# The last row tile of a normalised MLP output: another product order, its last product in two column halves, its store in quarters

## The chip, the cores and the metric

The kernel runs on one core of one Trainium2 chip. The metric is device time in microseconds (us) of one execution; lower is better. Five engines work side by side: TensorE (PE, matrix products, with its weight loads listed as PEld), VectorE (DVE), ScalarE (ACT), GpSimd (POOL) and SyncE (SP, which here issues transfers). Each takes its instructions in a fixed order and waits on semaphores that other engines or transfers raise. Products land in PSUM banks of 128 x 512 float32; the other tiles lie in SBUF. A row in this document that begins with a time, such as 1529.76, gives the start in us from the start of the profiled span.

## The reference, cut to what matters

Each of the DEPTH layers (one here) adds a token mixer and an MLP to x; then a last RMSNorm gives the output. Only the end bears on the change:

```python
def rms_norm(x, gain):
    xf = x.astype(jnp.float32)
    y = xf * lax.rsqrt(jnp.mean(xf * xf, axis=-1, keepdims=True) + NORM_EPS)
    return (y * gain.astype(jnp.float32)).astype(x.dtype)
...
        h = rms_norm(x, norm_mlp[l])
        x = x + jnp.square(jax.nn.relu(h @ w_up[l])) @ w_down[l]
    return rms_norm(x, norm_final)
```

x is 1024 x 1024 float32 (SEQ x D_MODEL), w_down is 4096 x 1024.

## The kernel before, in words

Rows of x are cut into eight row tiles of 128. The product of the MLP's hidden rows with w_down is not taken block by block: each 2 x 2 arrangement of blocks is computed with seven products in place of eight (Strassen's scheme in Winograd's form). A pair `pr` of row tiles, `pr` and `pr + 4`, is the upper and the lower half of such an arrangement; the two column halves of 512 are its other axis. `PLAN` names for each of the seven steps the PSUM bank that accumulates (X, Y or Z) and the two operands; `ADDS` says for each step into which column half `ci` and which row tile `pr + 4 * cj` VectorE then adds or subtracts the bank. Banks go on accumulating over steps: X is read after steps 0, 2, 4 and 6, Y after 1 and 5, Z after 3.

Every product is made of float32 operands split in a high and a low part: `mm3` issues three matmuls (lines 144, 145, 146) into the same bank. A step takes two blocks of the inner dimension, so six matmuls, each 128 x 512, for each row pair.

The inner dimension is walked in `n_kb` rounds of two blocks. The last round's second half (`alone`) takes its two pairs one after the other, pair 2 and then pair 3, all seven steps of each; before that, pairs go through the steps two at a time. Pair 3 (row tiles 3 and 7) thus comes last. In the order before, the last four additions of a pair (as `ADDS` has them) are, for pair 3, step 3 (Z into row 3, columns 0 to 511), step 4 (X into row 7, columns 512 to 1023), step 5 (Y into row 7, columns 0 to 511) and step 6 (X into row 3, columns 512 to 1023).

`finish(t, hf, whole)` is called when column half `hf` of row tile `t` is complete. At the first call for a row tile it multiplies that half by the final gain into `gx[:, 512:]` (line 1621, VectorE). At both calls ScalarE squares the half and sums it along the row (line 1624, with a read of the accumulator). At the second call (`whole`) VectorE adds the two sums (1626), ScalarE takes the root (1627), VectorE the reciprocal (1628); then VectorE scales the second half in place by reciprocal and gain (1629) while ScalarE scales the half that has its gain already (1632). ScalarE's queue issues the store of the one (1633), SyncE's the store of the other (1634), 256 KB each.

The order on each engine is made by the framework's list scheduler from the order of the code and its priorities; engines then keep to it. Waits are set by the framework from the tiles that an instruction reads and writes. All row tiles but rows 3 and 7 are stored while products of pair 3, or of pair 2, still run.

Of the kernel before, what the change touches and what calls it, by code (L numbers as in the profile page):

```python
# [18 lines left out]
P = 128  # L19
# [14 lines left out]
QUADS = 16  # L34
# [11 lines left out]
def trunk(ctx: ExitStack, tc: tile.TileContext, x, wts, mlp, pv, gains, mask_f, mask_u, out):  # L46
    nc = tc.nc
    V, A, G, PE = nc.vector, nc.scalar, nc.gpsimd, nc.tensor

    const = ctx.enter_context(tc.tile_pool(name="const", bufs=1))  # L50
# [11 lines left out]
    def bank(tag, name):  # L62
        return ps.tile([P, 512], F32, tag=tag, name=name, bufs={"pj": 4, "sc": 2, "hg": 2}[tag])
# [28 lines left out]
    def raw_tile(name):  # L92
        return wp.tile([P, 1024], F32, tag="raw", name=name, bufs=4)
# [44 lines left out]
    def pin(ins):  # L138
        if pinned[0]:
            tc.keep_in_program_order(ins)  # L140

    def mm3(o, ah, al, bh, bl, first, last, goes_on=False):
        how = {"skip_group_check": True} if goes_on else {}
        pin(PE.matmul(o, ah, bh, start=first, stop=False, **how))  # L144
        pin(PE.matmul(o, ah, bl, start=False, stop=False, **how))  # L145
        pin(PE.matmul(o, al, bh, start=False, stop=last, **how))  # L146
# [899 lines left out]
    for i in range(NC * NPAIR):  # L1046
# [398 lines left out]
    for part in range(2):  # L1445
# [4 lines left out]
        for hf in range(2):  # L1450
# [17 lines left out]
            for tt in tts:  # L1468
                cols = slice(hf * 512, (hf + 1) * 512)
# [36 lines left out]
    u_ops, last_u = {}, [None]  # L1506
# [70 lines left out]
    x2 = [(acc0, acc1)[t // 4].tile([P, D], F32, tag="acc", name=f"acc{t}", bufs=4) for t in range(8)]  # L1577
# [28 lines left out]
    for t in (0, 4, 1, 5, 2, 6, 3, 7):  # L1606
        nc.scalar.dma_start(x2[t], x2d[t])
    gain2 = gain_tile(2)
    ADDS = (
        ("X", 0, 0, ALU.add), ("Y", 1, 1, ALU.subtract), ("X", 0, 1, ALU.add), ("Z", 0, 0, ALU.add),  # L1610
        ("X", 1, 1, ALU.subtract), ("Y", 0, 1, ALU.add), ("X", 1, 0, ALU.subtract),
    )
    ssqs, with_gain = {}, {}

    def finish(t, hf, whole):

        cols = slice(hf * 512, (hf + 1) * 512)
        if t not in ssqs:
            ssqs[t] = const.tile([P, 2], F32, tag="ossq", name=f"ossq{t}", bufs=8)
            with_gain[t] = (raw_tile(f"gx{t}"), cols)  # L1620
            V.tensor_tensor(out=with_gain[t][0][:, 512:], in0=x2[t][:, cols], in1=gain2[:, cols], op=ALU.mult)
        ssq = ssqs[t]
        gx, cols_g = with_gain[t]
        A.activation(gx[:, 0:512], x2[t][:, cols], AF.Square, accum_out=ssq[:, hf : hf + 1])
        if whole:
            V.tensor_tensor(out=ssq[:, 0:1], in0=ssq[:, 0:1], in1=ssq[:, 1:2], op=ALU.add)
            A.activation(ssq[:, 0:1], ssq[:, 0:1], AF.Sqrt, bias=eps_t, scale=1.0 / D)
            V.reciprocal(ssq[:, 0:1], ssq[:, 0:1])
            V.scalar_tensor_tensor(
                x2[t][:, cols], x2[t][:, cols], ssq[:, 0:1], gain2[:, cols], op0=ALU.mult, op1=ALU.mult  # L1630
            )
            A.activation(gx[:, 512:], gx[:, 512:], AF.Identity, scale=ssq[:, 0:1])
            nc.scalar.dma_start(out[t * P : (t + 1) * P, cols_g], gx[:, 512:])
            nc.sync.dma_start(out[t * P : (t + 1) * P, cols], x2[t][:, cols])

    for kb in range(n_kb):
        last = kb + 1 == n_kb
        qs = order[2 * kb : 2 * kb + 2]
        for half in range(2):
            pairs = (2 * half, 2 * half + 1)  # L1640
            banks = {}
            if half == 1 and not last:
                nq = [QUADS + v for v in order[2 * kb + 2 : 2 * kb + 4]]
                for i in range(2):
                    load_quad(nq[i], raw_of[i], behind_late)
                    work[nq[i]] = quad_steps(nq[i], side[i][0], raw_of[i])
            alone = last and half == 1
            for step, (bk, wo, uo), prs in [
                (i, plan, prs) for prs in ([(pr,) for pr in pairs] if alone else [pairs]) for i, plan in enumerate(PLAN)
            ]:  # L1650
                first = (bk, prs[0]) not in banks
                for i, q in enumerate(qs):
                    wh, wl = ops_w[QUADS + q][wo]
                    uh, ul = u_ops[q][uo]
                    for pr in prs:
                        if first and i == 0:
                            banks[bk, pr] = bank(BANK[bk], f"d{bk}{kb}{pr}")
                        cut = slice(pr * P, (pr + 1) * P)
                        mm3(banks[bk, pr], uh[:, cut], ul[:, cut], wh, wl, first and i == 0, i == 1, not first)
                for pr in prs:  # L1660
                    _, ci, cj, op = ADDS[step]
                    dst = x2[pr + 4 * cj][:, ci * 512 : (ci + 1) * 512]
                    V.tensor_tensor(out=dst, in0=dst, in1=banks[bk, pr], op=op)  # L1663
# [90 lines left out]
```

## Time and profile before

| What | Before |
|---|---|
| time, median of 3 runs | 1540.57 us (1539.04 to 1540.85) |
| time of the profiled execution | 1539.23 us |
| its span | 1537.4 us |
| around the span | 1539.23 - 1537.4 = 1.83 us |
| PE busy | 1523.7 us, 99% of the span |
| VectorE, ScalarE busy | 1149.8 us (75%), 809.8 us (53%) |
| granted TensorE clock | 0.999 of full speed |
| start of the last product | 1529.33 us |

The span is what the profiler saw of the core, from its first to its last event; the time has 1.83 us more around it. A busy share is an average over the whole span. What happens after the last product is a stage of its own, in which PE does nothing; it is 1537.4 - 1529.33 = 8.1 us long, and it is read from the timeline, instruction by instruction, not from the shares.

### The profile page before, as it was taken

What the parts mean: (1) busy time and instruction counts of PE and PEld (TensorE: products, weight loads), DVE (VectorE), ACT (ScalarE), POOL (GpSimd) and SP (SyncE); (2) the same over time, 40 slices, a digit from 0 to 9 for tenths busy, and PEclk for the clock granted to TensorE, in tenths of its full rate; (3) what the DMA queues carried; (4) which work ended last, traced back from release to release, by engine and by line L of the source; (5) the groups of instructions that cost most, each with busy time, mean ns of one, the idle gap of its engine ahead of it and who ended that gap; (6) DMA issues with size and microseconds to landing.
All of it is one profiled execution on the core that took longest, in us unless ns stands there. A gap on an engine that the chain in (4) does not pass through costs nothing. (4 is left out here: it accounts for less than half of the span.)

```text
span 1537.4 us, 23195 instructions
## 1 busy us (share of the span) xinstructions
PE 1523.7 (99%) x9085; PEld 1274.5 (83%) x9085; DVE 1149.8 (75%) x1656; ACT 809.8 (53%) x1341; POOL 149.8 (10%) x188
## 2 busy tenths in 40 slices
PE   9999999999999999999999999999999999999997
PEld 7878988888889888888888888888888778888886
DVE  6798696485685838786856578888888898888877
ACT  6656757667567335454533357667776721111115
POOL 1021210232624600000000000000000000000000
PEclk9999999999999999999999999999999999999999
DMA  8545455465664374332339224766666675666642
GB/s 300 198 156 202 138 196 204 148 208 184 220 228 138 104 294 183 133 136 87 133 110 336 116 110 164 273 248 247 247 247 247 229 307 219 249 252 249 251 183 110
DMA packets 81679, 306.82 MB, mean 200 GB/s; under 512 B 8481, under 2 KB 20897, under 8 KB 68642
## 3 DMA queue, kind: packets, MB, share of 16 engines
q1 hardware_dynamic: 77536, 292.75, 51.8%
q10 hardware_dynamic: 4034, 12.59, 2.2%
q8 instruction: 71, 1.16, 0.3%
q14 instruction: 38, 0.31, 0.1%
HBM read 201.50 MB, written 103.81 MB: 199 GB/s over the span
## 5 line engine op out<-in xcount | busy, mean ns | idle before, releaser
L1663 DVE TENSOR_TENSOR acc<-acc,dX 128x512 f32<-128x512 f32 x128 | 85.2, 686 | 29.2 <-PE dX L146 26.7
L87 ACT CAST wA<-q 128x512 fp32r<-128x512 f32 x46 | 28.6, 621 | 146.6 <-PE dX L146 101.9
L88 DVE TENSOR_TENSOR wL<-raw,wH 128x1024 fp32r<-128x1024 f32 x46 | 56.3, 1226 | 41.1 <-ACT wH L87 40.8
L87 ACT CAST wH<-raw 128x1024 fp32r<-128x1024 f32 x46 | 48.2, 1050 | 34.4 <-DMA raw<-wts_in 14.3
L1663 DVE TENSOR_TENSOR acc<-acc,dY 128x512 f32<-128x512 f32 x64 | 43.5, 687 | 13.1 <-PE dY L146 12.9
L144 PE MATMUL po<-wH,y 128*128 128x512 f32 x128 | 49.9, 394 | 0.0
L145 PE MATMUL po<-wL,y 128*128 128x512 f32 x128 | 49.9, 390 | 0.0
L146 PE MATMUL po<-wH,y 128*128 128x512 f32 x128 | 49.7, 390 | 0.0
L1524 ACT ACTIVATE b<-b 128x512 f32<-128x512 f32 x48 | 30.2, 630 | 32.0 <-DVE b L1523 31.8
L88 DVE TENSOR_TENSOR wA<-q,wA 128x512 fp32r<-128x512 f32 x46 | 31.5, 687 | 16.2 <-ACT wA L87 15.8
L108 ACT CAST wH<-raw 128x1024 fp32r<-128x1024 f32 x36 | 37.7, 1048 | 8.3 <-issue 3.7
L569 DVE SCALAR_TENSOR_TENSOR xc<-xp,pvt,xc 128x512 f32<-128x512 f32 x48 | 40.2, 848 | 1.1 <-ACT xc L553 1.1
L175 POOL TENSOR_TENSOR rstd_h<-rstd_h,mhalf 128x1 f32<-128x1 f32 x8 | 4.6, 583 | 371.1 <-DVE rstd_h L170 371.1
L1085 DVE TENSOR_TENSOR s<-q,q 128x512 f32<-128x512 f32 x46 | 31.7, 688 | 3.9 <-DMA q<-mlp_in 3.5
L482 POOL TENSOR_TENSOR stt<-r,stt 128x256 fp32r<-128x256 f32 x16 | 19.8, 1261 | 126.4 <-ACT stt L481 114.2
L1093 DVE TENSOR_TENSOR s<-q 128x512 f32<-128x512 f32 x46 | 31.7, 688 | 0.4
L1525 ACT ACTIVATE b<-b 128x512 f32<-128x512 f32 x48 | 30.2, 631 | 1.2
L873 ACT ACTIVATE on<-po 128x128 f32<-128x128 f32 x64 | 16.8, 277 | 26.1 <-PE po L869 26.0
L146 PEld LDWEIGHTS po<-wH,y 128*128 128x128 f32 x128 | 24.0, 188 | 5.0
L144 PEld LDWEIGHTS po<-wH,y 128*128 128x128 f32 x128 | 24.1, 188 | 4.8
L145 PEld LDWEIGHTS po<-wL,y 128*128 128x128 f32 x128 | 24.1, 188 | 4.8
L1175 DVE TENSOR_TENSOR gb<-gY,ge 128x512 f32<-128x512 f32 x14 | 9.7, 691 | 23.6 <-PE gY L146 23.6
(2562 smaller groups left out, 5437.2 us busy)
## 6 DMA issues: line engine op xcount, KB each, us to landing
q<-mlp_in SPq DMA_DIRECT2D x92, 512.0 KB, 3.6
raw<-wts_in SPq DMA_DIRECT2D x80, 512.0 KB, 4.9
rest<-wL SPq DMA_DIRECT2D x36, 512.0 KB, 2.9
wL<-rest SPq DMA_DIRECT2D x36, 512.0 KB, 4.3
hd<-ri SPq DMA_DIRECT2D x16, 256.0 KB, 3.4
od<-onT ACTq DMA_DIRECT2D x8, 512.0 KB, 6.6
cdT<-stT SPq DMA_DIRECT2D x16, 256.0 KB, 3.1
o<-od SPq DMA_DIRECT2D x4, 1024.0 KB, 5.9
```

What stands on the lines that cost most here:

```text
L87: keep(A.copy(h, src))
L88: ins = V.tensor_tensor(out=lo, in0=src, in1=h.bitcast(F32), op=ALU.subtract)
L108: A.copy(h, raw)
L144: pin(PE.matmul(o, ah, bh, start=first, stop=False, **how))
L145: pin(PE.matmul(o, ah, bl, start=False, stop=False, **how))
L146: pin(PE.matmul(o, al, bh, start=False, stop=last, **how))
L569: ins = V.scalar_tensor_tensor(xc[:, s, :], xp[:, j : j + T], pvt[:, PV_CW + 8 * j + u : PV_CW + 8 * j + u + 1], xc[:, s, :], op0=ALU.mult ...
L1085: ins = V.tensor_tensor(out=sa[:, 0, :], in0=a21, in1=a22, op=ALU.add)
L1093: V.tensor_tensor(out=sb[:, 0, :], in0=a21, in1=a11, op=ALU.add)
L1524: A.activation(b[:, at, :], b[:, at, :], AF.Relu, scale=-1.0 if at == 2 else 1.0)
L1525: A.activation(b[:, at, :], b[:, at, :], AF.Square)
L1663: V.tensor_tensor(out=dst, in0=dst, in1=banks[bk, pr], op=op)
```

## The change

The change is in `finish` and in the last round's loop, and touches pair 3 alone (row tiles 3 and 7, the last ones):

- the steps of pair 3 run in the order 0, 1, 2, 4, 5, 3, 6: the two steps that complete row 7 (4 and 5) now stand ahead of step 3, which completes the first half of row 3;
- the last step, 6, is computed in two parts of 256 columns: six matmuls of 128 x 256 for columns 0 to 255 of the bank, an addition of 256 columns, a call of `finish`, and then the same for columns 256 to 511;
- `finish` with a `part` squares 256 columns only; the first part's sum is added to the sum of the row's other half in a tile of its own, `thirds`; the second part adds its own sum to that, and takes root and reciprocal;
- row 3 is then scaled and stored in four quarters of 256 columns (128 KB each): VectorE and ScalarE take a quarter each, twice; three of the stores are issued by SyncE, the fourth by ScalarE.

```diff
@@ finish
-        A.activation(gx[:, 0:512], x2[t][:, cols], AF.Square, accum_out=ssq[:, hf : hf + 1])
+        if part is None:
+            A.activation(gx[:, 0:512], x2[t][:, cols], AF.Square, accum_out=ssq[:, hf : hf + 1])
+        else:
+            if part == 0:
+                thirds[t] = const.tile([P, 2], F32, tag="thirds", name=f"thirds{t}", bufs=1)
+            now = slice(hf * 512 + part * 256, hf * 512 + part * 256 + 256)
+            o = thirds[t][:, 0:1] if part == 0 else ssq[:, hf : hf + 1]
+            A.activation(gx[:, part * 256 : part * 256 + 256], x2[t][:, now], AF.Square, accum_out=o)
+            if part == 0:
+                V.tensor_tensor(out=o, in0=o, in1=ssq[:, 1 - hf : 2 - hf], op=ALU.add)
+                return
         if whole:
-            V.tensor_tensor(out=ssq[:, 0:1], in0=ssq[:, 0:1], in1=ssq[:, 1:2], op=ALU.add)
+            other = ssq[:, 1 - hf : 2 - hf] if part is None else thirds[t][:, 0:1]
+            V.tensor_tensor(out=ssq[:, 0:1], in0=ssq[:, hf : hf + 1], in1=other, op=ALU.add)
             A.activation(ssq[:, 0:1], ssq[:, 0:1], AF.Sqrt, bias=eps_t, scale=1.0 / D)
             V.reciprocal(ssq[:, 0:1], ssq[:, 0:1])
+            if part is not None:
+                rows = slice(t * P, (t + 1) * P)
+                for i, dma in enumerate((nc.sync.dma_start, nc.scalar.dma_start)):
...
+                    V.scalar_tensor_tensor(
+                        x2[t][:, o], x2[t][:, o], ssq[:, 0:1], gain2[:, o], op0=ALU.mult, op1=ALU.mult
+                    )
+                    A.activation(gx[:, g], gx[:, g], AF.Identity, scale=ssq[:, 0:1])
+                    nc.sync.dma_start(out[rows, o], x2[t][:, o])
+                    dma(out[rows, o_g], gx[:, g])
+                return
@@ the loop of the last round
-                (i, plan, prs) for prs in ([(pr,) for pr in pairs] if alone else [pairs]) for i, plan in enumerate(PLAN)
+                (i, PLAN[i], prs)
+                for prs in ([(pr,) for pr in pairs] if alone else [pairs])
+                for i in ((0, 1, 2, 4, 5, 3, 6) if alone and prs[0] == 3 else range(7))
             ]:
+                if alone and prs[0] == 3 and step == 6:
+                    _, ci, cj, op = ADDS[step]
+                    for part in range(2):
+                        these = slice(part * 256, part * 256 + 256)
+                        o = banks[bk, 3][:, these]
...
+                            mm3(o, uh[:, cut], ul[:, cut], wh[:, these], wl[:, these], False, i == 1, True)
+                        dst = x2[3 + 4 * cj][:, ci * 512 + part * 256 : ci * 512 + part * 256 + 256]
+                        V.tensor_tensor(out=dst, in0=dst, in1=o, op=op)
+                        finish(3, ci, part == 1, part)
+                    continue
```

In the new file the addition of a bank stands in line 1703 (1663 before), that of a part in line 1689, the Square of a whole half in line 1625 and of a part in 1631, the sum for the root in 1637, the reciprocal in 1639, and row 3's quarter scalings in 1646 and 1649 with their stores in 1650 and 1651.

Every engine's instructions stand as before up to pair 3's last products. PE, the end of the program, before (dX, dY and dZ are the banks of pair 3; the operands named wA and ws are weights, u the hidden rows; a wait names the engine whose semaphore is awaited):

```order
L144 MATMUL dY_13595<-ws328H,u12B_13345 128x512
L145 MATMUL dY_13595<-ws328L,u12B_13345 128x512
L146 MATMUL dY_13595<-ws328H,u12B_13345 128x512
L144 MATMUL dY_13595<-ws329H,u13B_13353 128x512
L145 MATMUL dY_13595<-ws329L,u13B_13353 128x512
L146 MATMUL dY_13595<-ws329H,u13B_13353 128x512
L144 MATMUL dX_13587<-wA1228H,u12t_13347 128x512 [waits DVE_49]
L145 MATMUL dX_13587<-wA1228L,u12t_13347 128x512
L146 MATMUL dX_13587<-wA1228H,u12t_13347 128x512
L144 MATMUL dX_13587<-wA1229H,u13t_13355 128x512
L145 MATMUL dX_13587<-wA1229L,u13t_13355 128x512
L146 MATMUL dX_13587<-wA1229H,u13t_13355 128x512
```

PE, the same place now:

```order
L144 MATMUL dZ_13636<-wA1229H,u13B_13351 128x512
L145 MATMUL dZ_13636<-wA1229L,u13B_13351 128x512
L146 MATMUL dZ_13636<-wA1229H,u13B_13351 128x512
L144 MATMUL dX_13587<-wA1228H,u12t_13347 128x256 [waits DVE_49]
L145 MATMUL dX_13587<-wA1228L,u12t_13347 128x256
L146 MATMUL dX_13587<-wA1228H,u12t_13347 128x256
L144 MATMUL dX_13587<-wA1229H,u13t_13355 128x256
L145 MATMUL dX_13587<-wA1229L,u13t_13355 128x256
L146 MATMUL dX_13587<-wA1229H,u13t_13355 128x256
L144 MATMUL dX_13587<-wA1228H,u12t_13347 128x256 [waits DVE_49]
L145 MATMUL dX_13587<-wA1228L,u12t_13347 128x256
L146 MATMUL dX_13587<-wA1228H,u12t_13347 128x256
```

Z's products stand where Y's were; Y's have moved ahead of them. The last product's six matmuls have become twelve of half the width (the last three are not shown), and the second half's first one has a wait for VectorE: both halves lie in the bank dX_13587, and the semaphore count that it waits for is reached by VectorE's addition of the first half (L1689, below).

VectorE, the end of the program, before (acc_11405 is row tile 7, acc_11401 row tile 3, gx_13630 and gx_13619 their halves with gain, ossq_13629 and ossq_13618 their sums and scales):

```order
L1663 TENSOR_TENSOR acc_11401<-acc_11401,dZ_13610 128x512 [waits PE_49]
L1621 TENSOR_TENSOR gx_13619<-acc_11401,gain_11439 128x512 [waits DMAHW0_49,DVE_49]
L1663 TENSOR_TENSOR acc_11405<-acc_11405,dX_13587 128x512 [waits PE_49]
L1621 TENSOR_TENSOR gx_13630<-acc_11405,gain_11439 128x512 [waits DMAHW2_49,DVE_49]
L1663 TENSOR_TENSOR acc_11405<-acc_11405,dY_13595 128x512 [waits PE_49]
L1663 TENSOR_TENSOR acc_11401<-acc_11401,dX_13587 128x512 [waits PE_49]
L1626 TENSOR_TENSOR ossq_13629<-ossq_13629 128x1 [waits Activation_49]
L1626 TENSOR_TENSOR ossq_13618<-ossq_13618 128x1 [waits Activation_49]
L1628 RECIPROCAL ossq_13629<-ossq_13629 128x1 [waits Activation_49]
L1629 SCALAR_TENSOR_TENSOR acc_11405<-acc_11405,ossq_13629,gain_11439 128x512 [waits DVE_49]
L1628 RECIPROCAL ossq_13618<-ossq_13618 128x1 [waits Activation_49]
L1629 SCALAR_TENSOR_TENSOR acc_11401<-acc_11401,ossq_13618,gain_11439 128x512 [waits DVE_49]
```

VectorE, the same place now (ossq_13617 and gx_13618 are row 7's, ossq_13644 and gx_13645 row 3's):

```order
L1621 TENSOR_TENSOR gx_13618<-acc_11405,gain_11439 128x512 [waits DMAHW0_49,DVE_49]
L1703 TENSOR_TENSOR acc_11401<-acc_11401,dZ_13636 128x512 [waits PE_49]
L1637 TENSOR_TENSOR ossq_13617<-ossq_13617 128x1 [waits Activation_49]
L1689 TENSOR_TENSOR acc_11401<-acc_11401,dX_13587 128x256 [waits PE_49]
L1621 TENSOR_TENSOR gx_13645<-acc_11401,gain_11439 128x512 [waits DMAHW2_49,DVE_49]
L1639 RECIPROCAL ossq_13617<-ossq_13617 128x1 [waits Activation_49]
L1653 SCALAR_TENSOR_TENSOR acc_11405<-acc_11405,ossq_13617,gain_11439 128x512 [waits DVE_49]
L1633 TENSOR_TENSOR thirds_13655<-thirds_13655,ossq_13644 128x1 [waits Activation_49]
L1689 TENSOR_TENSOR acc_11401<-acc_11401,dX_13587 128x256 [waits PE_49]
L1637 TENSOR_TENSOR ossq_13644<-ossq_13644,thirds_13655 128x1 [waits Activation_49]
L1639 RECIPROCAL ossq_13644<-ossq_13644 128x1 [waits Activation_49]
L1646 SCALAR_TENSOR_TENSOR acc_11401<-acc_11401,ossq_13644,gain_11439 128x256 [waits DVE_49]
```

Both additions into row 7 (acc_11405) now come ahead of this piece. Between the two halves of row 3's last addition (L1689) VectorE now does the gain of row 3's first half, row 7's reciprocal, row 7's scaling (L1653) and the sum in `thirds`. One more quarter scaling follows the last row shown.

ScalarE, now, from row 7's second Square on:

```order
L1625 ACTIVATE gx_13645,ossq_13644<-acc_11401 128x512 [waits DMAHW2_49,DVE_49]
L1638 ACTIVATE ossq_13617<-ossq_13617,eps_t 128x1 [waits DVE_49]
L1631 ACTIVATE gx_13645,thirds_13655<-acc_11401 128x256 [waits DVE_49,Activation_49]
L1656 ACTIVATE gx_13618<-gx_13618,ossq_13617 128x512 [waits DVE_49]
L1657 DMA y_out<-gx_13618 128x512 [waits Activation_49]
L1631 ACTIVATE gx_13645,ossq_13644<-acc_11401 128x256 [waits DVE_49]
L1638 ACTIVATE ossq_13644<-ossq_13644,eps_t 128x1 [waits DVE_49]
```

Row 7's root, its scaling (L1656) and the issue of its store (L1657) stand ahead of the Square of row 3's second part; before, both rows' Squares stood ahead of both rows' roots.

More of the change, by code (lines that the diff above doesn't have):

```diff
@@ L1612, in trunk, with finish @@
     )
-    ssqs, with_gain = {}, {}
-    def finish(t, hf, whole):
+    ssqs, with_gain, thirds = {}, {}, {}
+    def finish(t, hf, whole, part=None):
         cols = slice(hf * 512, (hf + 1) * 512)
@@ L1623, in finish @@
         gx, cols_g = with_gain[t]
-        A.activation(gx[:, 0:512], x2[t][:, cols], AF.Square, accum_out=ssq[:, hf : hf + 1])
+        if part is None:
[9 more added lines that the diff above has]
+                return
         if whole:
-            V.tensor_tensor(out=ssq[:, 0:1], in0=ssq[:, 0:1], in1=ssq[:, 1:2], op=ALU.add)
+            other = ssq[:, 1 - hf : 2 - hf] if part is None else thirds[t][:, 0:1]
+            V.tensor_tensor(out=ssq[:, 0:1], in0=ssq[:, hf : hf + 1], in1=other, op=ALU.add)
             A.activation(ssq[:, 0:1], ssq[:, 0:1], AF.Sqrt, bias=eps_t, scale=1.0 / D)
             V.reciprocal(ssq[:, 0:1], ssq[:, 0:1])
+            if part is not None:
+                rows = slice(t * P, (t + 1) * P)
+                for i, dma in enumerate((nc.sync.dma_start, nc.scalar.dma_start)):
+                    g = slice(512 + 256 * i, 768 + 256 * i)
+                    o = slice(cols.start + 256 * i, cols.start + 256 * i + 256)
+                    o_g = slice(cols_g.start + 256 * i, cols_g.start + 256 * i + 256)
+                    V.scalar_tensor_tensor(
[5 more added lines that the diff above has]
+                return
             V.scalar_tensor_tensor(
@@ L1648, in trunk @@
             for step, (bk, wo, uo), prs in [
-                (i, plan, prs) for prs in ([(pr,) for pr in pairs] if alone else [pairs]) for i, plan in enumerate(PLAN)
+                (i, PLAN[i], prs)
+                for prs in ([(pr,) for pr in pairs] if alone else [pairs])
+                for i in ((0, 1, 2, 4, 5, 3, 6) if alone and prs[0] == 3 else range(7))
             ]:
                 first = (bk, prs[0]) not in banks
+                if alone and prs[0] == 3 and step == 6:
[3 more added lines that the diff above has]
+                        o = banks[bk, 3][:, these]
+                        for i, q in enumerate(qs):
+                            wh, wl = ops_w[QUADS + q][wo]
+                            uh, ul = u_ops[q][uo]
+                            cut = slice(3 * P, 4 * P)
+                            mm3(o, uh[:, cut], ul[:, cut], wh[:, these], wl[:, these], False, i == 1, True)
[3 more added lines that the diff above has]
+                    continue
                 for i, q in enumerate(qs):
```

## The prediction

> **What bounds the kernel now.** The page comes first: PE is busy in 99% of the span.
>
> ```profile
> span 1537.4 us, 23195 instructions
> PE 1523.7 (99%) x9085; PEld 1274.5 (83%) x9085; DVE 1149.8 (75%) x1656; ACT 809.8 (53%) x1341; POOL 149.8 (10%) x188
> ```
>
> The change neither removes nor adds column work on PE, so this share says nothing of it. What it touches is the stage behind the last products, and that is read from the timeline of the last 10 us (start, duration, engine, line, in square brackets the idle time and who ended it):
>
> ```profile
> 1529.33 0.39 PE L146 MATMUL dX<-wA1229H,u13t 128*128 128x512 f32 x1
> 1529.76 0.69 DVE L1663 TENSOR_TENSOR acc<-acc,dX 128x512 f32<-128x512 f32 x1 [0.67 <-PE dX L146]
> 1530.36 0.15 DVE L1626 TENSOR_TENSOR ossq<-ossq 128x1 f32<-128x1 f32 x1
> 1530.48 0.63 ACT L1624 ACTIVATE gx<-acc 128x512 f32<-128x512 f32 x1 [0.57 <-DVE acc L1663]
> 1531.01 0.19 ACT L1624 ACTIVATION_READ_ACCUMULATOR gx<-acc 128x1 f32 x1
> 1531.11 0.61 ACT L1627 ACTIVATE ossq<-ossq,eps_t 128x1 f32<-128x1 f32 x2
> 1531.23 0.16 DVE L1626 TENSOR_TENSOR ossq<-ossq 128x1 f32<-128x1 f32 x1 [0.72 <-ACT gx L1624]
> 1531.42 0.16 DVE L1628 RECIPROCAL ossq<-ossq 128x1 f32<-128x1 f32 x1
> 1531.62 0.75 DVE L1629 SCALAR_TENSOR_TENSOR acc<-acc,ossq,gain 128x512 f32<-128x512 f32 x1
> 1531.63 0.71 ACT L1632 ACTIVATE gx<-gx,ossq 128x512 f32<-128x512 f32 x1
> 1532.29 0.15 DVE L1628 RECIPROCAL ossq<-ossq 128x1 f32<-128x1 f32 x1
> 1532.37 0.37 ACTq L1633 DMA_DIRECT2D y_out<-gx  x1
> 1532.48 0.75 DVE L1629 SCALAR_TENSOR_TENSOR acc<-acc,ossq,gain 128x512 f32<-128x512 f32 x1
> 1532.78 0.72 ACT L1632 ACTIVATE gx<-gx,ossq 128x512 f32<-128x512 f32 x1 [0.45 <-DVE ossq L1628]
> 1533.54 0.34 ACTq L1633 DMA_DIRECT2D y_out<-gx  x1
> ```
>
> One sees a chain of single steps in which PE has no part: last addition, Square, root, reciprocal, and then two rows' scalings in a line, row 7's (1531.62) ahead of row 3's; the second reciprocal waits for VectorE to end row 7's scaling, and the second ScalarE scaling for the first one's issue as well. Last comes the transfer view of 1532.0 to 1537.4 (40 slices of 0.135 us, busy tenths of the transfer engines), and the stores' own view:
>
> ```profile
> DMA  0000000007999999999999999999400000000000
> DMA packets 576, 1.05 MB, mean 194 GB/s; under 512 B 64, under 2 KB 64, under 8 KB 576
> y_out<-gx ACTq DMA_DIRECT2D x1, 256.0 KB, 2.8
> L1634 SPq DMA_DIRECT2D y_out<-acc x8: 332/332/338, 1512.0 to 1533.3; - x8
> ```
>
> Four stores of 256 KB run in one block, slice 9 to slice 28, which is 1533.2 to 1535.9: 2.6 us, 0.8 us behind the first issue (1532.37). The last one, issued at 1533.54, has landed 2.8 us later, at 1536.34, 0.44 us behind the last bytes; the span ends 1.06 us after that. So the stage is bound twice: by the step chain up to 1533.54, and by 1 MB of stores that all start within it.
>
> **The change, term by term.** Up to the third X product of pair 3 every queue stands as before. From there:
>
> ```profile
> 1522.09 0.68 DVE L1663 TENSOR_TENSOR acc<-acc,dX 128x512 f32<-128x512 f32 x1
> 1523.17 0.39 PE L145 MATMUL dX<-ws128L,u12n 128*128 128x512 f32 x1
> 1524.08 0.39 PE L146 MATMUL dX<-ws129H,u13n 128*128 128x512 f32 x1
> 1524.31 0.39 PE L145 MATMUL dZ<-wA1228L,u12B 128*128 128x512 f32 x1
> 1524.51 0.69 DVE L1663 TENSOR_TENSOR acc<-acc,dX 128x512 f32<-128x512 f32 x1 [0.15 <-PE dX L146]
> 302.72 0.28 PE L145 MATMUL pv<-wL,hT10H 128*128 128x256 f32 x1
> 302.84 0.28 PE L146 MATMUL pv<-wH,hT10L 128*128 128x256 f32 x1
> ```
>
> PE, new order. Matmuls of 512 columns follow each other in 0.227 us (four steps from 1523.17 to 1524.08), those of 256 in 0.12 (302.72, 302.84). Twelve by 0.12 against six by 0.227 costs 1.44 - 1.36 = 0.08 us. A VectorE result releases PE 0.17 us after its end: 1522.09 + 0.68 = 1522.77, and the matmul behind the waiting one starts at 1523.17, one pitch after 1522.94. Four Y matmuls, in place of five Z ones, now fill the wait for the X addition that ends at 1524.51 + 0.69 = 1525.20; the next X matmul goes at 1525.37 instead of 1525.22, 0.15 late. Six X end their starts at 1526.50, two Y at 1526.96, five Z at 1528.09, six half-width ones at 1528.92; the first half's bank is complete at 1528.92 + 0.28 = 1529.20 and PE free at 1529.04.
>
> VectorE, the queue that decides. Rows for its pace:
>
> ```profile
> 1522.02 0.16 DVE L1626 TENSOR_TENSOR ossq<-ossq 128x1 f32<-128x1 f32 x1
> 1526.38 0.69 DVE L1621 TENSOR_TENSOR gx<-acc,gain 128x512 f32<-128x512 f32 x1
> 1527.04 0.69 DVE L1663 TENSOR_TENSOR acc<-acc,dX 128x512 f32<-128x512 f32 x1
> L664 DVE TENSOR_TENSOR dd<-sc,mf 128x256 f32<-128x256 f32 x8 | 3.4, 419 | 0.0
> L481 ACT CAST stT<-r 128x256 fp32r<-128x256 f32 x16 | 5.9, 416 | 0.7 <-POOL r L474 0.7
> ```
>
> Full-width additions follow at 0.66 us (1526.38, 1527.04), a sum of one column starts 0.60 behind an addition (1529.76, 1530.36), and an addition 0.07 behind such a sum (1522.02, 1522.09). Row 7's X addition can start at 1526.50 + 0.39 + 0.04 = 1526.93; Y's at 1527.59; the gain of row 7 at 1528.25; Z's addition at 1528.91; row 7's sum at 1529.51; the first half's addition at 1529.58, 0.42 long: 1530.00. PE, which waits for it since both halves lie in one bank, stands idle from 1529.04 to 1530.17 (1.13 us; behind the waiting matmul are only its five fellows), and has the second half ready at 1531.05. But VectorE isn't: the gain of row 3 (from 1529.93), row 7's reciprocal (1530.62; its root runs on ScalarE 1530.26 to 1530.55, behind the Square of row 3's first half), row 7's scaling (1530.82, 0.75) and the sum in `thirds` (1531.49) come first. The second half's addition runs 1531.56 to 1531.98. Before, the last addition ended at 1529.76 + 0.69 = 1530.45: **+1.53 us**. PE's wait is inside this; were it gone, row 7's work on VectorE would still end at the same time, so its price on the path is nothing.
>
> ScalarE. Row 7's scaling (1531.07 to 1531.78) and the issue of its store, which holds ScalarE 0.37 us (the [0.45] row above shows it), end at 1532.17; the last Square starts at 1532.21, not 1532.01: **+0.20**. A Square of 256 columns isn't in the trace; the cast of 256 took 0.416, the Square of 512 0.63, so it lies between 0.32 (half) and 0.63; I take 0.42, since cast and Square cost alike at 512 columns (0.62 and 0.63). Square start to scaling start took row 7 before 1531.62 - 1530.48 = 1.14 with its sum already made, and row 3 would have needed 1.46 (sum 0.19 more after 1531.23, root 0.31, reciprocal 0.20); less 0.21 it is 1.25: the first quarter's scaling starts at 1533.46. Row 3 before waited for row 7's scaling and started at 1532.48, 2.00 after its Square; here **-0.75**.
>
> Quarters. A 256-column scaling on VectorE lies between 0.38 (half) and 0.75; I take 0.48 (0.75 less the 0.27 that an addition saves, 0.69 to 0.42); on ScalarE 0.50. VectorE's end at 1533.93 and 1534.35, ScalarE's at 1533.96 and 1534.44. SyncE issues at 1533.95, 1534.30 and 1534.65 (0.33 each), ScalarE at 1534.47. The last issue starts 1.11 us later than the 1533.54 of before.
>
> Stores. Row 7's 512 KB are issued at 1531.6 and 1531.8 and are through by 1533.7, out of the way: this is what the new order buys. Row 3's four quarters begin at 1533.95 + 0.82 = 1534.77. Each has 128 rows of 1 KB, where the halves had 128 of 2 KB (512 such packets, 32 for each of 16 engines, in 2.62 us: 82 ns each). No row shows a 1 KB packet in this stage: it costs between 41 ns (bytes alone) and 82 ns. I take 41, because the block of before runs at 9 tenths throughout, as if bytes bound it: 32 packets by 41 ns is 1.31, last bytes at 1536.08, against 1535.9. **Sum: +0.2 us.** The span becomes 1537.6, this execution 1537.6 + 1.83 = 1539.4. The three runs' median is 1540.57, 1.34 above this execution; at the median I get 1540.8.
>
> [...] The trace has the last store's 2.8 us with three others ahead of it, and no lone quarter.
>
> **The rivals.** (1) *Faster*: the halves overlap and row 7 is out of the way, as the code is laid out. VectorE would then add the second half right behind the first, at 1530.42, and ScalarE take its Square at once: 1.56 + 0.20 sooner than above, last bytes at 1534.3, 1.6 before 1535.9. For it: ScalarE has 0.57 and 0.72 of idle time in the chain above. Against it: the rows of VectorE's queue, where four instructions of row 7 and row 3 stand between the halves, and PE's new wait, so the change does not do this. It gives 1537.6 in this execution, 1539.0 at the median. (2) *Slower*: a store's rows of 1 KB cost what rows of 2 KB do. Last bytes at 1534.77 + 2.62 = 1537.39, +1.5 us: 1540.7 here, 1542.1 at the median. It decides from 35 ns a packet on (1534.77 + 32 x 35 ns = 1535.9). For it: the fixed share of other small work here (256 columns cost 0.42 where 512 cost 0.69). (3) *Nothing at all*, the terms cancelling closer than I can reckon: 1540.57.
>
> **How the numbers follow.** The forecast and (3), which differ by 0.2 us, hold 0.65; (1), or a good part of it, 0.13; (2), or a good part, 0.22. About 0.2% (3.1 us) is what a measurement of this kernel can tell from no change, and the whole stage from the last product's start is 8.1 us; none of the cases leaves 0.2%. I leave 0.02 for faster and 0.04 for slower by more, for things outside this stage, so 0.94 for within. Bounds: the low ends (Square 0.32, scalings at half) save 0.2 on the way, the packet at 82 ns and full-width prices add 1.8; the runs of before lie 1.5 below and 0.3 above their median. The range takes (1) and (2) in: 1538.7 to 1542.5.
>
> **What would show it.** In the changed trace: PE idle near 1.1 us between the two halves, ended by VectorE's L1689; VectorE without a gap from 1526.9 to about 1532; row 7's scaling (L1653) ahead of the second L1689, which ends about 1.5 us later than 1530.45; the last issue near 1534.65; the block of four quarters 1.3 us long (2.6 in rival 2). If the second L1689 ends near 1530.5, rival 1 holds. If all ends before pair 3 have moved, the cause lies elsewhere and I am wrong altogether.

## The result, and the profile after

The changed kernel takes 1555.92 us (median of 4 runs, 1554.91 to 1557.12) against 1540.67 us of the kernel before (4 runs, 1539.04 to 1540.85): a ratio of 1.0101, 95% interval 1.0089 to 1.0113. It is 1.0% slower, by 15 us; the prediction had 1540.8 us and a range up to 1542.5. The profiled execution took 1556.85 us. Its page begins:

```profile
span 1555.0 us, 23218 instructions
PE 1539.8 (99%) x9091; PEld 1274.7 (82%) x9091; DVE 1152.3 (74%) x1659; ACT 811.3 (52%) x1344; POOL 153.7 (10%) x188
```

PE is busy 16.1 us longer (1523.7 before) with six matmuls more, and its share is still 99%. The granted clock is 0.999, as before. Outside its busy time PE has 1555.0 - 1539.8 = 15.2 us against 13.7, so waits are 1.5 us of the 17.6 us between the two spans. The rest is PE itself, slower at its work. (The two medians lie 15.25 us apart, the two profiled executions a little more.)

**The stage that was predicted.** To compare it I count from one instruction that is the same in both programs, the last X matmul ahead of the changed order (`dX<-ws129H,u13n`, line 146; 1524.08 before). In the timeline of the changed kernel:

```profile
1541.49 0.39 PE L146 MATMUL dX<-ws129H,u13n 128*128 128x512 f32 x1
...
1545.09 0.39 PE L144 MATMUL dZ<-wA1229H,u13B 128*128 128x512 f32 x1
1545.32 0.40 PE L145 MATMUL dZ<-wA1229L,u13B 128*128 128x512 f32 x1
1545.56 0.39 PE L146 MATMUL dZ<-wA1229H,u13B 128*128 128x512 f32 x1
...
1546.83 0.42 DVE L1689 TENSOR_TENSOR acc<-acc,dX 128x256 f32<-128x256 f32 x1
1547.30 0.39 PE L144 MATMUL dX<-wA1228H,u12t 128*128 128x256 f32 x1 [0.65 <-DVE acc L1689]
1548.02 0.75 DVE L1653 SCALAR_TENSOR_TENSOR acc<-acc,ossq,gain 128x512 f32<-128x512 f32 x1
1548.76 0.41 DVE L1689 TENSOR_TENSOR acc<-acc,dX 128x256 f32<-128x256 f32 x1
1549.23 0.42 ACT L1631 ACTIVATE gx<-acc 128x256 f32<-128x256 f32 x1 [0.42 <-DVE acc L1689]
1550.49 0.88 DVE L1646 SCALAR_TENSOR_TENSOR acc<-acc,ossq,gain 128x256 f32<-128x256 f32 x2
1551.90 0.45 SPq L1650 DMA_DIRECT2D y_out<-acc  x1
```

From the marker to the end of the span it was 1537.4 - 1524.08 = 13.32 us, and it is now 1555.0 - 1541.49 = 13.51: +0.19 us, where the prediction had +0.2. PE stands idle between the halves and VectorE ends the wait; row 7's scaling (1548.02) lies ahead of the second half's addition. All of it is there as told, and it is 1% of the loss. The marker itself starts 17.41 us later. Everything was lost before it, in code that the diff doesn't touch.

The transfers' view of the last 5.4 us of the changed kernel (40 slices of 0.135 us; moved GB/s below):

```profile
DMA  6999999899100000299459999999700000000000
GB/s 273 364 425 440 364 425 455 319 440 349 31 0 0 0 0 0 99 372 372 129 212 357 319 349 342 349 372 364 243 8 0 0 0 0 0 0 0 0 0 0
```

Row 7's stores are through before row 3's begin. Row 3's quarters are the block from slice 16 on: by the trace's packet records it runs from 1551.84 to 1553.58. There a packet of 1 KB takes 46 ns (median); one of 2 KB, in row 7's stores, takes 84.

**Where the time went.** The start of successive matmuls tells it: 1545.09, 1545.32, 1545.56 is a pitch of 0.235 us; before, 512 columns took 0.227. Windows of 200 us (columns: stretch, its length, PE busy and its matmuls, clock, share of the transfer engines, GB/s), of the kernel before, then of the changed one:

```profile
700.00:900.00 200.00, 200.00 (x908) 1.00 0.44 159
1300.00:1500.00 200.00, 200.00 (x884) 1.00 0.61 240
```

```profile
700.00:900.00 200.00, 200.00 (x891) 1.00 0.43 154
1300.00:1500.00 200.00, 200.00 (x872) 1.00 0.59 232
```

PE is busy without a gap at the same clock, and gets through 17 and 12 fewer matmuls. The transfers are not busier. Not every matmul is hit, though. Within one stage, the products into the bank gX (a row: line, operands, count, then shortest, median and longest duration in ns, first and last start), before and after:

```profile
L144 PE MATMUL gX<-gn2H,ws134H x4: 389/389/390, 561.8 to 563.9; 128*128 128x512 f32 x4
L144 PE MATMUL gX<-gT3H,ws334H x4: 389/389/390, 567.3 to 569.3; 128*128 128x512 f32 x4
```

```profile
L144 PE MATMUL gX<-gn2H,ws134H x4: 395/396/396, 562.7 to 564.8; 128*128 128x512 f32 x4
L144 PE MATMUL gX<-gT3H,ws334H x4: 389/389/390, 568.2 to 570.3; 128*128 128x512 f32 x4
```

Both weights lie in a pool on the left of SBUF. `gT3H` lies on the left too, `gn2H` in the pool `np`, which is opened with `side="right"`. Of these two only the product whose operands come from both sides has become slower. That points to where tiles lie. The diff makes one new tile, `thirds`, of 128 x 2 float32: 8 bytes in each partition. In the addresses of the compiled programs it takes 32 bytes in the pool `const`, and every pool that is opened on the left after it stands 32 bytes higher than before; the tiles on the right have not moved. Before, the start of the moving operand (512 columns) and that of the stationary one were a multiple of 512 bytes apart in all 512-column matmuls. Now 1872 of them have a distance of 32 bytes up or down of such a multiple. Pitch by stage, worked out from the starts in both traces (mean of the steps between successive 512-column matmuls, steps outside 0.20 to 0.26 us left out), and the count of matmuls times the difference:

| Products into | Matmuls | Before, ns | After, ns | Difference, us |
|---|---|---|---|---|
| pr, pi, g, mb (before 550 us) | 384 | 227.6 | 227.6 | 0.0 |
| gX, gY, gZ | 672, 336, 168 | 226.8, 226.7, 226.7 | 228.5, 230.2, 228.6 | 2.6 |
| po (820 to 918 us) | 384 | 226.9 | 230.3 | 1.3 |
| uX, uY, uZ | 768, 384, 192 | 227.1, 226.7, 226.9 | 233.3, 233.4, 233.3 | 8.5 |
| dX, dY, dZ | 768, 384, 192 | 226.9, 226.7, 227.0 | 230.2, 230.0, 229.5 | 4.3 |

The sum is 16.7 us, against 17.4 us by which the marker is late. PE's longer gaps are not in this sum, and they differ from profile to profile, by some 2.5 us in this case: the kernel before with an unused tile, of experiment 1, has the same pitches to 0.1 ns, and its marker, at 1539.03, is 14.95 us late. The products into dX, dY and dZ are slower too, though both operands of each come from one side; more of that below.

### The profile page after: what moved, and what is told of

Read it like the earlier page. It is cut to its first block, busy times and chain, and to the rows that moved or that the text cites. A ratio compares the mean times of both kernels' runs of the same rounds, so it can differ in the third digit from the quotient of the medians.

```text
span 1555.0 us, 23218 instructions
## 1 busy us (share of the span) xinstructions
PE 1539.8 (99%) x9091; PEld 1274.7 (82%) x9091; DVE 1152.3 (74%) x1659; ACT 811.3 (52%) x1344; POOL 153.7 (10%) x188
## 4 chain that ended last, share of the span: by engine, by line
PE 88%; DVE 7%; DMA 2%; issue 1%; ACT 1%; POOL 1%; SPq 0%; DVEq 0%; ACTq 0%
PE uX L144 4%; PE uX L145 4%; PE uX L146 4%; PE dX L144 3%; PE dX L146 3%; PE dX L145 3%; PE gX L144 3%; PE gX L145 3%; PE gX L146 3%; PE po L145 2%; PE po L146 2%; PE po L144 2%; PE pj_q L144 2%; PE uY L146 2%; PE uY L145 2%; PE uY L144 2%
## 5 line engine op out<-in xcount | busy, mean ns | idle before, releaser
L87 ACT CAST wH<-raw 128x1024 fp32r<-128x1024 f32 x46 | 48.2, 1048 | 34.1 <-DMA raw<-wts_in 15.2
L88 DVE TENSOR_TENSOR wA<-q,wA 128x512 fp32r<-128x512 f32 x46 | 31.6, 688 | 17.4 <-ACT wA L87 17.4
```

What stands on the lines that cost most here:

```text
L87: keep(A.copy(h, src))
L88: ins = V.tensor_tensor(out=lo, in0=src, in1=h.bitcast(F32), op=ALU.subtract)
```

## The experiments

The theory (**placement**): the new tile, not the new work, costs the 15 us, because it changes how the two operands of a matmul lie to each other. The rival (**work**): the new order, halves or quarters disturb something earlier. The ratios are against the kernel before on the same chip, and 0.2% is about what can be told from nothing.

**1. The tile alone, and the tile at another size.** The kernel before with an unused tile of 8 bytes in the same pool, no instruction changed; and the changed kernel with `thirds` at 64 bytes. The first form of the theory was that each operand's own start has to be a multiple of 64.

```diff
@@ before, ahead of finish
+    const.tile([P, 2], F32, tag="thirds", name="thirds3", bufs=1)
```

> The kernel before with one unused tile of 8 bytes a partition added to the same pool, no instruction changed. Placement theory: about 1555.7 us (1540.67 + 15.25 - 0.2), with the slower matmul spacing of the changed kernel (0.233 us in the stage that writes uX, uY, uZ). Tail theory: 1540.7 us.

Measured: 1555.37 us (4 runs), ratio 1.0096 (1.0081 to 1.0111).

```diff
@@ after
-                thirds[t] = const.tile([P, 2], F32, tag="thirds", name=f"thirds{t}", bufs=1)
+                thirds[t] = const.tile([P, 16], F32, tag="thirds", name=f"thirds{t}", bufs=1)
```

> The changed kernel with nothing but the tile thirds widened from 8 to 64 bytes a partition, so that the tiles behind it move by 64 bytes instead of 32. Placement theory (the 15 us come from tiles that lie 32 bytes off, not from the new instructions): the median goes back to the kernel before plus the +0.2 us of the last rows, about 1540.9 us, and 512-column matmuls follow each other in 0.227 us again in every stage. Tail theory (the new order, halves and quarters cost the time): 1555.9 us as before this repair, since no instruction changes.

Measured: 1555.6 us (4 runs), ratio 1.0099 (1.0084 to 1.0114). The groups of the products into uX, by line, shape and operands (matmuls; busy us, mean ns of one; idle time ahead): the kernel before, the changed one, before with the unused tile, changed with 64 bytes:

```profile
L144 PE MATMUL uX<-h2B11H,wA 128*128 128x512 f32 x64 | 25.0, 391 | 0.0
```

```profile
L144 PE MATMUL uX<-h2B11H,wA 128*128 128x512 f32 x64 | 25.4, 397 | 0.0
```

```profile
L144 PE MATMUL uX<-h2B11H,wA 128*128 128x512 f32 x64 | 25.4, 397 | 0.0
```

```profile
L144 PE MATMUL uX<-h2B11H,wA 128*128 128x512 f32 x64 | 25.4, 397 | 0.0
```

The unused tile costs 14.35 us with all instructions as before, within the intervals the same as the whole change: the rival of work falls. But 64 bytes are as bad as 8, though every start is then a multiple of 64 again. The first form of placement falls too.

**2. The distance between the sides.** Line 1127 has a spacer below the right-hand tiles, a tile that nothing reads. Its size moves the right side alone, so the distance can be set. The first of these stands for the second form of the theory: both operands at one place modulo 64. In the second the sides are 32 bytes apart again, but now it is the right one that lies off a multiple of 64.

```diff
@@ line 1127
-    pad.tile([P, 56], F32, tag="pad", name="pad")
+    pad.tile([P, 64], F32, tag="pad", name="pad")
```

In the changed kernel, where each operand then starts 32 bytes past a multiple of 64 and the sides are 64 bytes apart:

> The changed kernel with the spacer of the right-hand side of SBUF widened from 224 to 256 bytes, so that the right-hand tiles lie 32 bytes off too and both operands of every 512-column matmul start at the same remainder of 64 bytes (32 and 32). Placement theory in its relative form (a matmul is slow where its two operands' remainders differ): about 1541 us, spacing 0.227 us in all stages. In its absolute form (any operand that starts 32 bytes off costs): 1556 us or more, all 5780 matmuls of 512 columns slow, up to 1540.9 + 5780 x 6.6 ns = 1579 us. Tail theory: 1555.9 us.

Measured: 1555.1 us (4 runs), ratio 1.0098 (1.0081 to 1.0115). In the kernel before (no new tile; 32 bytes apart):

> The kernel before with only that spacer widened from 224 to 256 bytes: left-hand tiles on a multiple of 64 bytes, right-hand ones 32 off, so the remainders differ in the same matmuls as in the changed kernel, with the parts of the operands exchanged. Relative form: about 1556 us, 1680 matmuls of the stages gX, gY, uX, uY, uZ slow. Absolute form with the cost on the stationary operand alone: nearly 1540.7 us, since the stationary operands of those stages now lie on 64; with the cost on the moving operand alone: slow in those same stages, which the changed kernel (moving operand on 64 there) would then not be.

Measured: 1554.56 us (4 runs), ratio 1.0092 (1.0077 to 1.0107). Both are slow. By the first, sharing a place modulo 64 isn't enough; by the second it doesn't matter which side lies off. What is left is the distance itself. With 48 columns in the spacer of the changed kernel, both sides have moved by 32 bytes, every operand of the 512-column matmuls lies 32 bytes from where it lay, and the distance is a multiple of 512 again:

> The changed kernel with the right-hand spacer narrowed from 224 to 192 bytes: right-hand tiles move up by the same 32 bytes as the left-hand ones, so every operand lies 32 bytes from where it lay before, and the distance between moving and stationary operand is again a multiple of 512 bytes in all 5780 matmuls of 512 columns. Distance theory (a matmul is slow where moving and stationary operand differ modulo some power of two of at least 128 bytes): 0.227 us in all stages and 1540.9 us, that is the kernel before plus the +0.2 us of the last rows. Place theory (any tile off its old place costs, for instance against the transfers or the other engines): about 1555 us like the four others.

Measured: 1540.04 us (11 runs, 1539.02 to 1542.73), ratio 1.0004 (0.9995 to 1.0013). The 15 us are gone, with all of the change's work in place. Next, 24 columns in the kernel before, 128 bytes apart:

> The kernel before with that spacer narrowed from 224 to 96 bytes: the distance becomes 128 or 384 modulo 512 in the same 1872 matmuls that were off in the others. Distance theory with a modulus of 128: 1540.7 us. With 256 or 512: about 1555 us, the stages uX, uY, uZ at 0.233 us. Place theory: about 1555 us.

Measured: 1552.23 us (4 runs), ratio 1.0083 (1.0069 to 1.0096); the uX stage has a pitch of 232.6 ns. A multiple of 128 isn't enough either.

**3. The distance by itself.** A small kernel that computes nothing of the reference: 29 groups of 40 matmuls of 128 x 512, all operands in one large tile (declared float32r, as those of the products in the table above), the moving operand m bytes and the stationary one s bytes past a multiple of 512. No other engine works beside a group but for one copy of 8 columns at its end.

> The disputed cost by itself: this kernel computes nothing of the reference, it only runs 29 groups of 40 matmuls (128x128 by 128x512, float32r, another stationary block each time) out of one SBUF tile, with the moving operand m and the stationary operand s bytes from bases that are a multiple of 512 apart, no other engine working on PE's tiles. Distance theory: 0.227 us a matmul for m - s = 0, 512, 1024 and for (m, s) = (32, 32), (64, 64), (256, 256), (16, 16), whatever the place; about 0.233 us for the distances 32 to 480 up to the modulus (0.227 at 128, 256, 384 if it is 128; at 256 if it is 256). Place theory: the same spacing in all groups, since nothing else runs beside them.

The copies mark the ends of the groups, so the steps between them are the groups' lengths (start, duration; in brackets VectorE's wait for PE):

```profile
32.71 0.17 DVE L44 COPY res<-warm 128x8 f32<-128x8 f32 x1 [27.95 <-PE warm L39]
41.77 0.17 DVE L48 COPY res<-s 128x8 f32<-128x8 f32 x1 [8.90 <-PE s L39]
51.11 0.17 DVE L48 COPY res<-s 128x8 f32<-128x8 f32 x1 [9.17 <-PE s L39]
60.27 0.17 DVE L48 COPY res<-s 128x8 f32<-128x8 f32 x1 [9.00 <-PE s L39]
69.60 0.17 DVE L48 COPY res<-s 128x8 f32<-128x8 f32 x1 [9.16 <-PE s L39]
78.93 0.17 DVE L48 COPY res<-s 128x8 f32<-128x8 f32 x1 [9.16 <-PE s L39]
...
106.97 0.17 DVE L48 COPY res<-s 128x8 f32<-128x8 f32 x1 [9.16 <-PE s L39]
116.06 0.17 DVE L48 COPY res<-s 128x8 f32<-128x8 f32 x1 [8.93 <-PE s L39]
```

The first group, m = 0, takes 41.77 - 32.71 = 9.06 us, the next (m = 32) 9.34, m = 64 9.16, m = 96 and 128 9.33 each, and m = 256 (the last step shown) 9.09. By the starts of the matmuls, in ns each (s = 0 unless given):

| Distance m - s, bytes | Pitch, ns |
|---|---|
| 0, 256, 512, 1024 | 226.7, 227.3, 227.3, 226.7 |
| 0 with m = s = 32, 64, 256 | 226.8, 227.2, 226.7 |
| 64, 320 | 229.2, 229.2 |
| 32, 96, 128, 192, 224, 288, 352, 384, 448, 480 | 233.2 to 233.4 |
| 160, 416 | 234.4 |
| 4, 16 | 236.6, 231.8 |

In these groups the distance modulo 256 decides: 32 bytes cost 3% (233.2 to 233.4 against 226.7), 64 one percent (229.2), 256 (227.3) and both operands shifted alike by 32, 64 or 256 (226.7 to 227.2) nothing beyond the noise. The direction counts: m = 0 with s = 64 is a distance of -64, or 192 modulo 256, and takes 233.3 where 64 takes 229.2. This fits the two kernels above with sides 64 bytes apart, which were as slow as those with 32: by the addresses, 1680 of their 1872 products lie at -64. The last group repeats m = 0 and gave 227.3 for 226.7, so 0.6 ns is noise. At 62 to 66 and 70 to 74 us, within the groups m = 96 and 128, the clock is 1.00, VectorE, ScalarE and GpSimd are busy 0.00 us and the transfer engines' share is 0.00, so the cost needs neither another engine nor a lower clock. With both operands 16 bytes past, distance 0, it is 230.1: this one start off a multiple of 32 has a cost of its own. Why the distance matters is not shown.

**4. The modulus in the whole kernel.** If 256 is right, the kernel before with its sides 256 bytes apart must be as fast as at 512.

```diff
@@ line 1127
-    pad.tile([P, 56], F32, tag="pad", name="pad")
+    pad.tile([P, 120], F32, tag="pad", name="pad")
```

> The kernel before with one number changed: the spacer below the right-hand tiles has 120 columns (480 bytes) in place of 56 (224), so that the start of every moving operand lies 256 bytes off a multiple of 512 from its stationary operand's where the two come from different sides. Theory A, from the sweep: what counts is the distance modulo 256, so the spacing of the 512-column matmuls stays at 227 ns in every stage and the time at 1540.5 +- 1.5 us. Theory B (rival): the distance counts modulo 512, the sweep's 227.3 ns at 256 being a special case of two small tiles: the spacing in the stages with both sides rises to 233 ns and the time to 1552 to 1556 us.

Measured: 1541.17 us (10 runs), ratio 1.0007 (0.9997 to 1.0016), and a pitch of 226.7 to 227.1 ns in every stage from gX on. The group of uX in the changed kernel with 48 columns of spacer, and in this one:

```profile
L144 PE MATMUL uX<-h2B11H,wA 128*128 128x512 f32 x64 | 25.0, 390 | 0.0
```

```profile
L144 PE MATMUL uX<-h2B11H,wA 128*128 128x512 f32 x64 | 25.0, 390 | 0.0
```

Theory A holds.

**5. The parts of the change.** These were made to see what each part does to the tail. The kernel before with the new order alone (no new tile):

```diff
@@ the loop of the last round
-                (i, plan, prs) for prs in ([(pr,) for pr in pairs] if alone else [pairs]) for i, plan in enumerate(PLAN)
+                (i, PLAN[i], prs)
+                for prs in ([(pr,) for pr in pairs] if alone else [pairs])
+                for i in ((0, 1, 2, 4, 5, 3, 6) if alone and prs[0] == 3 else range(7))
```

> The kernel before with the new order of the last pair's products alone: the last product whole, row 3 scaled and stored whole, no new tile. By the distance theory no matmul spacing moves and the time is 1540.5 +- 1.5 us. Tail, from the marker matmul (the last dX product ahead of the changed order) to the end of the span: 13.32 us in the kernel before. By the prediction's own terms it is 12.8 us (-0.5: the product's last accumulation ends later, but the last row's division is already through). Rival: the order alone is what costs the 15 us (a stage ahead of the tail is delayed by it): 1555 us.

Measured: 1539.44 us (10 runs), ratio 0.9998 (0.9989 to 1.0008). The same with row 3 scaled and stored in quarters (the last product whole):

```diff
@@ finish, in the branch for a complete row
+            if t == 3:
+                rows = slice(t * P, (t + 1) * P)
...
+                    nc.sync.dma_start(out[rows, o], x2[t][:, o])
+                    dma(out[rows, o_g], gx[:, g])
+                return
```

> As t1, and row 3 scaled and stored in quarters; the last product is still whole, and no new tile. Time 1540.5 +- 1.5 us. Tail from the marker to the end of the span: 12.9 us by the prediction's terms (four smaller stores whose last starts earlier, but with packets of 1 KB). Rival (packets of 1 KB cost as much as those of 2 KB): 14.4 us.

Measured: 1540.25 us (10 runs), ratio 1.0001 (0.9991 to 1.001). And halves and quarters in the old order, with the spacer at 48:

```diff
@@ after, the loop of the last round (and line 1127 with 48)
-                for i in ((0, 1, 2, 4, 5, 3, 6) if alone and prs[0] == 3 else range(7))
+                for i in range(7)
```

> The changed kernel with the order of before (halves and quarters kept) and the spacer of 48 columns, so the distance is a multiple of 512 as in e5. Time 1540.5 +- 1.5 us. Tail from the marker to the end of the span between 13.3 and 14.0 us: the halves' wait for VectorE stays, and the reordering's gain is gone. Rival: the halves cost nothing and the new order carried the tail's +0.2: 13.3 us or less.

Measured: 1540.05 us (10 runs), ratio 1.0002 (0.9992 to 1.0011). By time all three are the kernel before. Rows of their timelines: the marker, the last addition, row 3's scaling and, for the first, its last issue; first the order alone, then halves in the old order, then the changed kernel with the spacer at 48:

```profile
1523.76 0.39 PE L146 MATMUL dX<-ws129H,u13n 128*128 128x512 f32 x1
1529.76 0.68 DVE L1665 TENSOR_TENSOR acc<-acc,dX 128x512 f32<-128x512 f32 x1
1532.28 0.75 DVE L1629 SCALAR_TENSOR_TENSOR acc<-acc,ossq,gain 128x512 f32<-128x512 f32 x1
1533.04 0.37 ACTq L1633 DMA_DIRECT2D y_out<-gx  x1
```

```profile
1525.19 0.39 PE L146 MATMUL dX<-ws129H,u13n 128*128 128x512 f32 x1
1531.68 0.42 DVE L1689 TENSOR_TENSOR acc<-acc,dX 128x256 f32<-128x256 f32 x1
1532.21 0.75 DVE L1653 SCALAR_TENSOR_TENSOR acc<-acc,ossq,gain 128x512 f32<-128x512 f32 x1
1533.67 0.88 DVE L1646 SCALAR_TENSOR_TENSOR acc<-acc,ossq,gain 128x256 f32<-128x256 f32 x2
```

```profile
1524.93 0.39 PE L146 MATMUL dX<-ws129H,u13n 128*128 128x512 f32 x1
1531.45 0.75 DVE L1653 SCALAR_TENSOR_TENSOR acc<-acc,ossq,gain 128x512 f32<-128x512 f32 x1
1532.19 0.41 DVE L1689 TENSOR_TENSOR acc<-acc,dX 128x256 f32<-128x256 f32 x1
1533.92 0.88 DVE L1646 SCALAR_TENSOR_TENSOR acc<-acc,ossq,gain 128x256 f32<-128x256 f32 x2
```

Counted from the marker, in us, one profile each (the two copies of the change differ by 0.06 at the end of the span):

| Kernel | Last addition ends | Row 3's scaling starts | Last issue | Span ends |
|---|---|---|---|---|
| before | 6.37 | 8.40 | 9.46 | 13.32 |
| order alone | 6.68 | 8.52 | 9.28 | 13.14 |
| order and quarters | 6.67 | 8.52 | 10.08 | 12.96 |
| halves and quarters, old order | 6.91 | 8.48 | 9.92 | 13.11 |
| the change, spacer 48 | 7.67 | 8.99 | 10.41 | 13.57 |
| the change | 7.68 | 9.00 | 10.41 | 13.51 |

Order alone was expected at 12.8 and gave 13.14, order and quarters at 12.9 and gave 12.96. Halves in the old order were expected at 13.3 to 14.0 and gave 13.11, on the side of that run's rival, by which the halves cost nothing. In the old order VectorE adds the second half (1531.68) ahead of row 7's scaling (1532.21); in the new order row 7's scaling comes first, and the addition is 0.76 us later. By these single profiles it is the two together that cost about half a microsecond; either alone costs nothing that one profile can show.

## Why the prediction was wrong

The step that failed is the first one of its sum: "Up to the third X product of pair 3 every queue stands as before." The instructions stand as before, and from that I took it that their durations do. They don't: the tile `thirds`, for which the sum has no term at all, moves the left-hand operands by 32 bytes, and products with operands from both sides then take 233 ns in place of 227 (uX, uY and uZ: 233.3 to 233.4 against 226.7 to 227.1). The chance of 0.04 for slower by more than 0.2% "for things outside this stage" was the whole room that was left for this. The text's own test, ends that have moved before pair 3, is what happened.

The trace of before couldn't show it, since all its distances are multiples of 512 bytes. The code held a hint: a spacer tile that no instruction reads.

Inside the stage, by the terms of the prediction, in the changed kernel counted from the marker:

- The sum: +0.2 predicted, +0.19 measured (+0.25 with the spacer at 48). Right, but in part by luck: the steps below came up to 0.4 us sooner than forecast and the block of stores was 0.4 us longer, and the two cancelled.
- PE's wait between the halves: 1.13 us predicted, 0.65 measured. VectorE ended it as told, but 0.16 us sooner (first half's addition ends at 1547.25 - 1541.49 = 5.76, against 5.92), and the profile counts the wait from the end of the last matmul (1546.37 + 0.28 = 1546.65), not from PE's being free. Priced at nothing, and the two orders above agree: VectorE's queue decides.
- The second half's addition: 7.90 predicted (1531.98), 7.68 measured. Row 7's scaling stood in its way as told.
- Row 3's first scaling: 9.38 predicted, 9.00 measured; the last issue 10.57 predicted, 10.41 measured. The 256-column costs were close: Square 0.42 as taken, two scalings 0.88 on VectorE and 0.91 on ScalarE where 0.96 and 1.00 were taken.
- The four quarters: predicted as a block of 1.31 us, from 10.69 to 12.00; measured 1.75 us, from 10.35 to 12.09. The issues are 0.90 us apart from first to last where 0.70 was forecast, and a packet of 1 KB took 46 ns where 41 was taken. So the last bytes came 0.1 us behind the forecast's. Rival 2 did not happen: its price for 1 KB was that of 2 KB, 82 ns. The four quarters landed 2.0 to 2.2 us after their issue (the groups of the transfers' view).
- Rival 1 didn't happen: the halves don't overlap.

The products into dX, dY and dZ rose to 230 ns although both operands of each come from one side, at a multiple of 512 bytes. Their order changes from side to side, mostly every six products, and the starts of the changed kernel show that the cost hangs on these changes. The 222 steps at a change take 229.9 ns one way and 234.9 the other; the first five steps behind a change take 229.7 on average, between 224 and 241; the 69 steps that lie seven or more behind one take 227.1, as before (227.2). With the sides 256 or 512 bytes apart all take 227 (226.7 to 227.1 in experiment 4, 226.7 to 227.0 before). So here the cost goes with the distance between the operands of successive products, and one change delays several products. One change from right to left, 0.24 us long, with the load of the next product's weights:

```profile
1541.49 0.39 PE L146 MATMUL dX<-ws129H,u13n 128*128 128x512 f32 x1
1541.50 0.19 PEld L144 LDWEIGHTS dY<-ws328H,u12B 128*128 128x128 f32 x1
1541.73 0.39 PE L144 MATMUL dY<-ws328H,u12B 128*128 128x512 f32 x1
```

The next weights are loaded (0.19 us from 1541.50) while the product runs (0.39 us from 1541.49). Whether a matmul's own weights count or those loaded beside it isn't shown, since in the products into uX, uY and uZ both have one distance; nor is why a change is felt for several products.

## What to carry to other kernels

A new tile of 8 bytes moved the left-hand tiles behind it by 32 bytes: when a stage that the diff doesn't touch changes its pace, compare operand addresses before looking for a wait. On products of 512 columns with float32r operands, keep the starts of moving and stationary operands a multiple of 256 bytes apart (226.7 to 227.3 ns in the sweep with starts at multiples of 32, 229.2 to 236.6 at the other distances), those of successive products too (dX, dY and dZ: 229.5 to 230.2 in the changed kernel, 226.7 to 227.0 before). Here a spacer of another size between the two sides did it. To put small tiles where they push only one another is a proposal that was not tried.

## What the hardware showed that I had not expected

- In the sweep (one profile) the pitch of 128 x 512 matmuls depends on the operands' distance: 226.7 to 227.3 ns at 0 modulo 256 bytes (230.1 with both starts 16 bytes past), 229.2 at 64, 233.2 to 234.4 at the other multiples of 32, 231.8 at 16, 236.6 at 4. On this kernel it is 15 us of 1540.
- The busy share and the clock don't show it: PE is 99% busy at 0.999 in both kernels. The count of matmuls in a window (908 against 891) and the duration of one (389 against 396 ns) do.
- A store's packet of 1 KB took 46 ns and one of 2 KB 84 (medians, changed kernel): per byte the small one is 10% dearer, not twice.
- A change from operands on one side to operands on the other, 32 bytes off, slows the products for about six steps (in dX, dY and dZ of the changed kernel 229.7 ns in the five behind it, 227.1 from the seventh on).
